# Splitting the mixed attention values a unit later, from tiles loaded a unit ahead, and one decay row loaded later

## The chip, the cores and the metric

One NeuronCore of a Trainium2 chip runs the whole program. The metric is the device time of one execution in microseconds; the kernel before takes 1137.94 us (median of three runs, 1137.45 to 1139.55).

## The reference, cut to what matters

One decoder layer on 1024 tokens of width 1024. Eight heads of kind A attend in a sliding window, eight heads of kind B attend causally with a decay bias; both read one input projection, and both results go through one output projection. A squared-ReLU MLP follows.

```python
xn = rmsnorm(x, attn_norm_g)
proj = einsum('bsd,de->bse', xn, w_in)            # q, k, v of both kinds, forget logits
out_a = swa_sinks_attention(qa, ka, va, sinks)     # 8 heads, window 128
c = cumsum(log_sigmoid(f_logit + b_forget))        # one decay row of 1024 values per B head
p = softmax(causal(qb @ kb.T * scale + c[q] - c[k]))
out_b = p @ vb                                     # 8 heads
x = x + concat([out_a, out_b]) @ w_out
x = x + square(relu(rmsnorm(x) @ w_up)) @ w_down
```

## The kernel before

**Arithmetic.** Every matmul operand is split in two parts, high and low, and three products (high-high, high-low, low-high) stand for one. `split` (line 73) makes the parts: ACT casts the high part, POOL or DVE subtracts it.

**Stages.** (1) The projection of the first columns; (2) attention: eight A heads in 16 units of work, then the B heads in pairs p = 0 to 3, eight units each (u = 0 to 3 the first head of the pair, 4 to 7 the second); (3) the output projection; (4) the up products and the down products of the MLP. This change lies in stage 2 from the B heads on and in the first products of stage 3.

**A unit.** `scores_b` (line 604) makes the score products (`spb`) on PE, adds the decay row (`cb`) on DVE (line 626) and takes the exponential on ACT. `mix_b` (line 650) comes two units later (`DEPTH` = 2): PE transposes the probabilities (`tpb`), ACT and DVE evict them as `pth` (line 359) and `ptl` (line 360), PE multiplies them by the values (`pvb`), and DVE adds the two halves of the sum into `mtb` (line 679). For p < 3 the sum is not yet divided by its softmax denominator and goes to DRAM (`mix_d`). For p = 3 it is divided before and split directly into `mix7`.

**Mixed values.** `split_mix(e)` (line 556) finishes one pair e of the concatenated heads: for each half c of 512 tokens SP loads the sum (`mixr`) and the inverse denominators (`mixn`), DVE multiplies them (line 565), ACT and POOL split the product (`mixs`), and SP writes the parts to `mixs_d`. `SPLITS` (line 49) says behind which unit (p, u) each of the seven pairs e = 0 to 6 is started. `load_mix(e)` (line 777) reads a finished pair back as `mix0` to `mix6` for the output projection. Each of `mixr`, `mixn` and `mixs` has one buffer.

**Fillers.** The projections of later pairs (`ps` products) and the first halves of the output projection (`out_first`, `po` products of `mix0` to `mix3`) are laid between the units by `PACE`. After the last unit the program loads pair 6, multiplies pairs 4, 5 and 6 (lines 831 to 835), finishes the last two units (`drain(0)`) and multiplies pair 7. `out_finish` then adds the first halves and makes the operands of the MLP.

**Order.** The kernel is built with a scheduler that orders each engine's instructions by dependencies and priorities; each engine then runs its list in order, SP's list of transfers too. Inside `with tc.issue_after(i)` an instruction is placed behind i on its engine. `prep` gives a high priority.

**Decay rows.** `prep_k(p, h)` (line 594) makes the keys of head h and loads its decay row `cb`; it is called for h = 1 at the last unit of the pair before. There are two buffers of `cb`.

Of the kernel before, what the change touches and what calls it, by code (L numbers as in the profile page):

```python
# [8 lines left out]
F32 = mybir.dt.float32  # L9
# [3 lines left out]
ALU = mybir.AluOpType  # L13
# [3 lines left out]
P = 128  # L17
D = 1024
S = 1024
KT = D // P  # L20
NT = S // P
HD = 64
# [31 lines left out]
def hybrid_layer(  # L54
# [501 lines left out]
    def split_mix(e):  # L556

        for c in range(2):
            cs = slice(c * 512, (c + 1) * 512)
            m, q = (ap2.tile([P, 512], F32, tag=n, name=n, bufs=1) for n in ("mixr", "mixn"))  # L560
            hl = ap2.tile([P, 2, 512], F32R, tag="mixs", name="mixs", bufs=1)
            nc.sync.dma_start(m, mix_d[e][:, cs])
            for h in range(2):
                nc.sync.dma_start(q[rows_of[h], :], rd_d[2 * e + h, cs].partition_broadcast(HD))
            nc.vector.tensor_tensor(out=m, in0=m, in1=q, op=ALU.mult)
            split(hl[:, 0], hl[:, 1], m, nc.scalar, nc.gpsimd)
            nc.sync.dma_start(
                mixs_d[e][:, :, cs].rearrange("c p s -> p c s"), hl.bitcast(F32)
            )

# [23 lines left out]
    def prep_k(p, h):  # L594
        heads[p, "k1", h] = make_k_b(qkb[p], P, p, h)
        cb = ap2.tile([P, S], F32, tag="bias", name=f"cb{p}{h}", bufs=2)
        nc.sync.dma_start(cb, c_d[2 * p + h].partition_broadcast(P))
        heads[p, "cb", h] = cb
# [51 lines left out]
    def mix_b(probs, p, qp, h):  # L650
# [28 lines left out]
        nc.vector.tensor_tensor(out=mt[r, :], in0=pv[:HD, :256], in1=tmp[:, :256], op=ALU.add)  # L679
# [53 lines left out]

    def heads_b(p):
        for u in range(8):
            qp, h = (ORDER_END if p == 3 and u > 3 else ORDER_B)[u % 4], u // 4
            unit(lambda: scores_b(p, qp, h), lambda got, qp=qp, h=h: mix_b(got, p, qp, h))
            if u == DEPTH:
                prep(prep_v, p, 1)
                if p:  # L740
                    prep(inverse_to, 6 + 2 * p, dn_b[(p - 1) % 2], 2)
                else:
                    prep(inverse_a)
            if (p, u) in SPLITS:
                split_mix(SPLITS.index((p, u)))
            ahead(p + 1, u)
            fill()
# [191 lines left out]
    def up(j):  # L939
# [3 lines left out]
        s = slot(("m5", "m4")[j % 2], "wus", [4, 4, P])  # L943
# [180 lines left out]
    def h_add(c, dt, cs):  # L1124

        nset[1] += 1
        h = slot(("m3", "m5")[nset[1] % 2], "hy", [4, 512])
# [117 lines left out]
```

## Time and profile before

| | us |
|---|---|
| runs of before | 1137.94 median (1137.45 to 1139.55) |
| the profiled execution | 1135.57 |
| its span | 1133.8 |
| PE busy | 1105.2 (97%) |
| DVE busy | 767.8 (68%) |
| ACT busy | 574.4 (51%) |
| POOL busy | 383.4 (34%) |

The profiled execution is 2.4 us under the median. A busy PE is not a PE at its rate: a matmul that starts alone shows its whole latency as busy, one in a stream overlaps with the next, so the number of PE instructions in equal stretches says more than the busy share. The stretch that matters here runs from 215 us, where the first inverse denominators are ready, to 465 us, where the output projection begins to run without waits.

### The profile page before, as it was taken

How to read it: one execution, taken by the hardware profiler on the slowest of the kernel's cores; microseconds unless marked ns; L12 is line 12 of the kernel's file. 1: busy time of each engine (PE TensorE's matmuls, PEld its weight loads, DVE VectorE, ACT ScalarE, POOL GpSimd, SP SyncE). 2: the span in 40 equal slices, each digit the busy share in tenths (PEclk: the TensorE clock that was granted, in tenths of full speed). 3: DMA queues.
4: the chain of work that ended last, by engine and by line, in shares of the span. 5: the costliest groups of instructions: out<-in, count | busy, mean ns of one | idle time of the engine just before them, and what ended most of it. 6: DMA issues, size and time to landing. Idle time of an engine off the chain costs nothing.

```text
span 1133.8 us, 15566 instructions
## 1 busy us (share of the span) xinstructions
PE 1105.2 (97%) x5551; PEld 937.0 (83%) x5551; DVE 767.8 (68%) x1307; ACT 574.4 (51%) x1013; POOL 383.4 (34%) x342
## 2 busy tenths in 40 slices
PE   9999999989999999999999999999999999999998
PEld 8999987888997887787888887888888888888876
DVE  7476665766558577798867677856575877674493
ACT  5567567666557666545454534344443433333330
POOL 5751513345324634133332322222222222231241
PEclk9999999999999999999999999999999999999999
DMA  9311301355307647363554544335699786665441
GB/s 314 117 43 29 94 20 54 94 170 167 105 27 294 196 166 258 124 231 130 186 195 168 194 149 154 141 119 200 227 391 347 265 303 233 230 232 183 167 149 38
DMA packets 95710, 195.68 MB, mean 173 GB/s; under 512 B 7136, under 2 KB 19088, under 8 KB 95632
## 3 DMA queue, kind: packets, MB, share of 16 engines
q1 hardware_dynamic: 95488, 194.66, 49.0%
q8 instruction: 44, 0.72, 0.3%
q14 instruction: 34, 0.28, 0.1%
q10 hardware_dynamic: 144, 0.02, 0.0%
HBM read 141.61 MB, written 53.04 MB: 172 GB/s over the span
## 4 chain that ended last, share of the span: by engine, by line
PE 75%; DVE 9%; DMA 6%; issue 5%; POOL 3%; ACT 2%; SPq 0%; DVEq 0%; POOLq 0%; ACTq 0%
PE pd L71 27%; PE pu L71 26%; PE ps L71 6%; PE po L71 5%; PE qps L71 3%; DMA mixr<-mix_d 2%; PE pvb L71 2%; PE spb L71 2%; DVE ptl L360 1%; DMA h_d<-h 1%; PE sp L71 1%; PE tpb L662 1%; DVE sb L626 1%; POOL qkb L267 1%; DVE ss L241 1%
## 5 line engine op out<-in xcount | busy, mean ns | idle before, releaser
L71 PE MATMUL pd<-hx,wx 128*128 128x512 f32 x1344 | 306.8, 391 | 2.4 <-POOL wx L78 2.4
L71 PEld LDWEIGHTS pd<-hx,wx 128*128 128x128 f32 x1344 | 253.4, 189 | 55.7 <-POOL wx L78 2.8
L71 PE MATMUL pu<-bh,wu 128*128 128x512 f32 x896 | 281.9, 395 | 0.8 <-ACT bh L858 0.8
L71 PEld LDWEIGHTS pu<-bh,wu 128*128 128x128 f32 x896 | 168.3, 188 | 41.9 <-ACT bh L858 1.3
L71 PE MATMUL pu<-bl,wu 128*128 128x512 f32 x448 | 176.8, 395 | 0.1
L78 POOL TENSOR_TENSOR wx<-wda,wx 128x1024 fp32r<-128x1024 f32 x28 | 85.0, 3038 | 221.5 <-ACT wx L75 193.9
L75 ACT CAST hx<-hr 128x1024 fp32r<-128x1024 f32 x56 | 59.0, 1054 | 181.0 <-PE pd L71 175.8
L78 DVE TENSOR_TENSOR hx<-hr,hx 128x1024 fp32r<-128x1024 f32 x56 | 76.0, 1364 | 81.4 <-ACT hx L75 81.2
L71 PE MATMUL ps<-wh,xh 128*128 128x384 f32 (+1 forms) x320 | 110.3, 345 | 0.3 <-ACT qkb L582 0.3
L71 PE MATMUL ps<-wh,xl 128*128 128x384 f32 (+1 forms) x320 | 109.1, 342 | 0.0
L71 PE MATMUL ps<-wl,xh 128*128 128x384 f32 (+1 forms) x320 | 109.0, 341 | 0.0
L71 PEld LDWEIGHTS pu<-bl,wu 128*128 128x128 f32 x448 | 84.2, 188 | 21.0 <-DVE bl L78 0.8
L71 PE MATMUL po<-mix,wos 128*128 128x512 f32 x384 | 96.6, 398 | 2.3 <-ACT mix L75 0.8
L78 POOL TENSOR_TENSOR wu<-wus,wu 128x512 fp32r<-128x512 f32 x32 | 46.6, 1458 | 134.3 <-ACT wu L75 128.5
L71 PEld LDWEIGHTS po<-mix,wos 128*128 128x128 f32 x384 | 70.0, 188 | 17.6 <-ACT mix L75 1.5
L75 ACT CAST wu<-wus 128x512 fp32r<-128x512 f32 x64 | 39.0, 618 | 83.9 <-PE pu L71 75.7
L78 POOL TENSOR_TENSOR wu<-wur,wu 128x512 fp32r<-128x512 f32 x32 | 45.9, 1436 | 88.4 <-ACT wu L75 88.4
L926 DVE TENSOR_TENSOR ht<-hb 128x512 f32<-128x512 f32 x32 | 21.8, 722 | 67.0 <-ACT hb L981 67.0
L78 POOL TENSOR_TENSOR wl<-wr,wh 128x384 fp32r<-128x384 f32 (+1 forms) x47 | 50.0, 1075 | 50.0 <-ACT wh L75 38.6
L360 DVE TENSOR_TENSOR ptl<-tpb,pth 128x512 fp32r<-128x512 f32 (+1 forms) x80 | 50.2, 632 | 19.6 <-ACT pth L359 18.5
L75 ACT CAST wx<-wda 128x1024 fp32r<-128x1024 f32 x56 | 58.3, 1044 | 6.9 <-DMA wda<-in_w_d_dram 6.6
L71 PEld LDWEIGHTS ps<-wh,xh 128*128 128x128 f32 x320 | 60.4, 189 | 1.4 <-ACT qkb L582 0.6
(213 smaller groups left out, 2056.3 us busy)
## 6 DMA issues: line engine op xcount, KB each, us to landing
wda<-in_w_d_dram SPq DMA_DIRECT2D x34, 1024.0 KB, 8.5
hr<-hid_d SPq DMA_DIRECT2D x56, 512.0 KB, 5.8
wur<-in_w_u_dram SPq DMA_DIRECT2D x32, 512.0 KB, 4.4
hid_d<-ht SPq DMA_DIRECT2D x16, 1024.0 KB, 4.3
hid_d<-hb SPq DMA_DIRECT2D x16, 768.0 KB, 3.6
mixs_d<-mixs SPq DMA_DIRECT2D x14, 512.0 KB, 3.5
mix<-mixs_d SPq DMA_DIRECT2D x7, 1024.0 KB, 8.2
wr<-in_w_b_dram SPq DMA_DIRECT2D x32, 192.0 KB, 2.6
```

Of the source, the lines that this page charges most:

```text
L71: return nc.tensor.matmul(out, lhsT, rhs, start=start, stop=stop)
L75: hi_eng.copy(hi, src)
L78: lo_eng.tensor_tensor(out=lo, in0=src, in1=hi.bitcast(F32), op=ALU.subtract)
L241: nc.vector.tensor_reduce(out=ss, in_=sq[:, : n * w].rearrange("p (g d) -> p g d", d=HD), axis=AX.X, op=ALU.add,)
L267: nc.gpsimd.tensor_tensor(out=xt, in0=xt, in1=rv[:, t].unsqueeze(2).to_broadcast([P, na, HD]), op=ALU.mult)
L360: nc.vector.tensor_tensor(out=lo[:, cols], in0=pt[:, cols], in1=hi[:, cols].bitcast(F32), op=ALU.subtract)
L626: nc.vector.tensor_tensor_reduce(out=pr[:, c * 512 : c * 512 + n], in0=sp[:, :n], in1=cb[:, c * 512 : c * 512 + n], scale=1.0, scalar=3e38 ...
L662: nc.tensor.transpose(tp[:, c0 : c0 + P], probs[qi][:, kb * P : (kb + 1) * P], ident)
L926: eng.tensor_tensor(out=out, in0=a, in1=b, op=ALU.subtract)
```

## The change

`split_mix(e)` now returns three steps. `load` runs behind the unit of `SPLITS` and loads both halves, each into tiles of its own (two buffers of `mixr` and of `mixn`). `make(0)` runs behind the next unit and `make(1)` behind the one after; each multiplies, splits and writes one half, and the multiply is placed behind the sum `mtb` that was programmed last (`mixed[-1]`). `load_c(p, 1)`, the decay row of a pair's second head, moves from the last unit of the pair before to unit 1 of its own pair. Two later scratch tiles (`wus` of even j, one of the two `hy`) move to the pool `zr`, which opens after attention.

```diff
--- before.py
+++ after.py
@@ -555,18 +555,36 @@
 
     def split_mix(e):
 
-        for c in range(2):
-            cs = slice(c * 512, (c + 1) * 512)
-            m, q = (ap2.tile([P, 512], F32, tag=n, name=n, bufs=1) for n in ("mixr", "mixn"))
+
+        got = {}
+
+        def load():
+            for c in range(2):
+                cs = slice(c * 512, (c + 1) * 512)
+                m, q = got[c] = [
+                    ap2.tile([P, 512], F32, tag=n, name=n, bufs=2) for n in ("mixr", "mixn")
+                ]
+                nc.sync.dma_start(m, mix_d[e][:, cs])
+                for h in range(2):
+                    nc.sync.dma_start(
+                        q[rows_of[h], :], rd_d[2 * e + h, cs].partition_broadcast(HD)
+                    )
+
+        def make(c):
+            m, q = got[c]
             hl = ap2.tile([P, 2, 512], F32R, tag="mixs", name="mixs", bufs=1)
-            nc.sync.dma_start(m, mix_d[e][:, cs])
-            for h in range(2):
-                nc.sync.dma_start(q[rows_of[h], :], rd_d[2 * e + h, cs].partition_broadcast(HD))
-            nc.vector.tensor_tensor(out=m, in0=m, in1=q, op=ALU.mult)
+            with tc.issue_after(mixed[-1]):
+                nc.vector.tensor_tensor(out=m, in0=m, in1=q, op=ALU.mult)
             split(hl[:, 0], hl[:, 1], m, nc.scalar, nc.gpsimd)
             nc.sync.dma_start(
-                mixs_d[e][:, :, cs].rearrange("c p s -> p c s"), hl.bitcast(F32)
-            )
+                mixs_d[e][:, :, c * 512 : (c + 1) * 512].rearrange("c p s -> p c s"),
+                hl.bitcast(F32),
+            )
+
+        return [load, lambda: make(0), lambda: make(1)]
+
+
+    mixed = []
 
     def project_b(p):
         got = {}
@@ -593,9 +611,12 @@
 
     def prep_k(p, h):
         heads[p, "k1", h] = make_k_b(qkb[p], P, p, h)
-        cb = ap2.tile([P, S], F32, tag="bias", name=f"cb{p}{h}", bufs=2)
+        if h == 0:
+            load_c(p, 0)
+
+    def load_c(p, h):
+        cb = heads[p, "cb", h] = ap2.tile([P, S], F32, tag="bias", name=f"cb{p}{h}", bufs=2)
         nc.sync.dma_start(cb, c_d[2 * p + h].partition_broadcast(P))
-        heads[p, "cb", h] = cb
 
     def prep_v(p, h):
         c0 = 256 + h * HD
@@ -676,7 +697,10 @@
         tmp = ap2.tile([HD, 512], F32, tag="cmb", name="tmpb", bufs=1)
         nc.scalar.copy(tmp[:, :256], pv[HD:, :256])
         mt = ap2.tile([P, 256], F32, tag="mt", name="mtb", bufs=2)
-        nc.vector.tensor_tensor(out=mt[r, :], in0=pv[:HD, :256], in1=tmp[:, :256], op=ALU.add)
+        add = nc.vector.tensor_tensor(
+            out=mt[r, :], in0=pv[:HD, :256], in1=tmp[:, :256], op=ALU.add
+        )
+        mixed.append(add.ins)
         ms = slice(qp * 256, (qp + 1) * 256)
         if p < 3:
             nc.sync.dma_start(mix_d[4 + p, r, ms], mt[r, :])
@@ -731,18 +755,25 @@
                     prep(make_q_a, 1, g, j)
             fill()
 
+    splitting = []
+
     def heads_b(p):
         for u in range(8):
             qp, h = (ORDER_END if p == 3 and u > 3 else ORDER_B)[u % 4], u // 4
             unit(lambda: scores_b(p, qp, h), lambda got, qp=qp, h=h: mix_b(got, p, qp, h))
+            if u == 1:
+                load_c(p, 1)
             if u == DEPTH:
                 prep(prep_v, p, 1)
                 if p:
                     prep(inverse_to, 6 + 2 * p, dn_b[(p - 1) % 2], 2)
                 else:
                     prep(inverse_a)
+            for step in [st.pop(0) for st in splitting if st]:
+                step()
             if (p, u) in SPLITS:
-                split_mix(SPLITS.index((p, u)))
+                splitting.append(split_mix(SPLITS.index((p, u))))
+                splitting[-1].pop(0)()
             ahead(p + 1, u)
             fill()
 
@@ -940,7 +971,7 @@
         if 0 < j < NJ - 1:
             up_load(j + 1)
         raw = raws.pop(j)
-        s = slot(("m5", "m4")[j % 2], "wus", [4, 4, P])
+        s = slot(*(("m4", "wus", [4, 4, P]), ("m5", "wus", [4, 4, P], F32, "zr"))[j % 2 == 0])
         a11, a12, a21, a22 = raw[:, 0, :4], raw[:, 0, 4:], raw[:, 1, :4], raw[:, 1, 4:]
         plus(s[:, 0], a21, a22)
         minus(s[:, 1], s[:, 0], a11)
@@ -1124,7 +1155,7 @@
     def h_add(c, dt, cs):
 
         nset[1] += 1
-        h = slot(("m3", "m5")[nset[1] % 2], "hy", [4, 512])
+        h = slot(*(("m3", "hy", [4, 512]), ("m5", "hy", [4, 512], F32, "zr"))[nset[1] % 2])
         nc.sync.dma_start(h, h_d[dt : dt + 4, :, cs].rearrange("t p s -> p t s"))
         r = rr[:, cs].unsqueeze(1).to_broadcast([P, 2, 512])
         for d in (slice(0, 2), slice(2, 4)):
```

From `h<-po0` (line 868, now 899) on, all engines have their instructions in the same order as before; DVE, ACT and PE differ only between the first `mixr` and that place.

**DVE, units 6 and 7 of pair 0.** The rows from the first square sums (`ss`) of the next pair's normalisation on; `rqk` is the last of its chain, line 626 is now 647. Before:

```order
L241 TENSOR_REDUCE ss<-sq 128x16
L360 TENSOR_TENSOR ptl<-tpb,pth 128x512
L565 TENSOR_TENSOR mixr<-mixr,mixn 128x512
L246 SCALAR_TENSOR_TENSOR ss<-ss,ep_77 128x16
L626 ISA sb,nmb<-spb,cb_2295 128x512
L626 ISA nmb 128x1
L360 TENSOR_TENSOR ptl<-tpb,pth 128x512
L253 TENSOR_TENSOR su<-sr_2942 128x16
L626 ISA sb,nmb<-spb,cb_2295,nmb 128x384
L626 ISA nmb 128x1
L360 TENSOR_TENSOR ptl<-tpb,pth 128x384
```

Now:

```order
L241 TENSOR_REDUCE ss<-sq 128x16
L360 TENSOR_TENSOR ptl<-tpb,pth 128x512
L246 SCALAR_TENSOR_TENSOR ss<-ss,ep_77 128x16
L253 TENSOR_TENSOR su<-sr_2937 128x16
L254 TENSOR_TENSOR su<-su,ss 128x16
L261 SCALAR_TENSOR_TENSOR rqk<-su,sr_2937 128x4x4
L647 ISA sb,nmb<-spb,cb_2467 128x512
L647 ISA nmb 128x1
L360 TENSOR_TENSOR ptl<-tpb,pth 128x512
L360 TENSOR_TENSOR ptl<-tpb,pth 128x384
L647 ISA sb,nmb<-spb,cb_2467,nmb 128x384
```

No multiply stands inside the chain any more: the nearest one, of pair 0, follows the next sum `mtb`, twenty rows below the square sums. The four rows of the chain now follow each other.

**DVE and PE, the end of attention.** `mtb_5627` (before `mtb_5632`) is the sum of the third unit from the end, `mixr_5432` the second half of pair 6, `mix7` the split of the last pair. DVE before:

```order
L360 TENSOR_TENSOR ptl_5621<-tpb_5616,pth_5620 128x384
L360 TENSOR_TENSOR ptl_5669<-tpb_5664,pth_5668 128x384
L360 TENSOR_TENSOR ptl_5691<-tpb_5685,pth_5690 128x512
L679 TENSOR_TENSOR mtb_5632<-pvb_5576,tmpb_5630 64x256
L360 TENSOR_TENSOR ptl_5704<-tpb_5698,pth_5703 128x512
L679 TENSOR_TENSOR mtb_5680<-pvb_5663,tmpb_5678 64x256
L78 TENSOR_TENSOR mix7_4282<-mtb_5632,mix7_4282 64x256
L360 TENSOR_TENSOR ptl_5716<-tpb_5711,pth_5715 128x384
L78 TENSOR_TENSOR mix7_4282<-mtb_5680,mix7_4282 64x256
L679 TENSOR_TENSOR mtb_5727<-pvb_5684,tmpb_5725 64x256
```

DVE now:

```order
L360 TENSOR_TENSOR ptl_5616<-tpb_5611,pth_5615 128x384
L360 TENSOR_TENSOR ptl_5669<-tpb_5664,pth_5668 128x384
L360 TENSOR_TENSOR ptl_5691<-tpb_5685,pth_5690 128x512
L700 TENSOR_TENSOR mtb_5627<-pvb_5571,tmpb_5625 64x256
L577 TENSOR_TENSOR mixr_5432<-mixr_5432,mixn_5433 128x512
L360 TENSOR_TENSOR ptl_5704<-tpb_5698,pth_5703 128x512
L700 TENSOR_TENSOR mtb_5680<-pvb_5663,tmpb_5678 64x256
L78 TENSOR_TENSOR mix7_4282<-mtb_5627,mix7_4282 64x256
L360 TENSOR_TENSOR ptl_5716<-tpb_5711,pth_5715 128x384
L78 TENSOR_TENSOR mix7_4282<-mtb_5680,mix7_4282 64x256
L700 TENSOR_TENSOR mtb_5727<-pvb_5684,tmpb_5725 64x256
L78 TENSOR_TENSOR mix7_4282<-mtb_5727,mix7_4282 64x256
```

The second multiply of pair 6 now follows the sum of unit (3, 5); before it stood 46 rows ahead of that sum, and the first one 60 rows ahead.

PE before, where the products of pair 6 stand:

```order
L71 MATMUL pvb_5512<-pth_5518,vb31_5118 128x256
L71 MATMUL pvb_5512<-ptl_5519,vb31_5118 128x256
L71 MATMUL pvb_5512<-pth_5530,vb31_5118 128x256
L71 MATMUL po0_5643<-mix6_5636,wos_5640 128x512 x2
L71 MATMUL po1_5644<-mix6_5636,wos_5640 128x512 x2
L71 MATMUL po0_5643<-mix6_5636,wos_5640 128x512
L71 MATMUL po1_5644<-mix6_5636,wos_5640 128x512
L662 MATMUL tpb_5590<-ident_58,sb_5337 128x128 x2
L662 MATMUL tpb_5590<-ident_58,sb_5352 128x128 x2
L71 MATMUL pvb_5512<-ptl_5531,vb31_5118 128x256
```

PE now:

```order
L71 MATMUL pvb_5684<-pth_5715,vb31_5118 128x256
L71 MATMUL pvb_5684<-ptl_5716,vb31_5118 128x256
L71 MATMUL pvb_5684<-pth_5715,vb31_5118 128x256
L71 MATMUL pvb_5684<-ptl_5716,vb31_5118 128x256
L71 MATMUL po0_5643<-mix6_5636,wos_5640 128x512 x2
L71 MATMUL po1_5644<-mix6_5636,wos_5640 128x512 x2
L71 MATMUL po0_5643<-mix6_5636,wos_5640 128x512
L71 MATMUL po1_5644<-mix6_5636,wos_5640 128x512
L71 MATMUL po0_5643<-mix7_4282,wos_5640 128x512 x2
L71 MATMUL po1_5644<-mix7_4282,wos_5640 128x512 x2
L71 MATMUL po0_5643<-mix7_4282,wos_5640 128x512
L71 MATMUL po1_5644<-mix7_4282,wos_5640 128x512
```

The six products of pair 6 stood among the last units' transposes; now they stand behind the last `pvb` product, straight ahead of those of pair 7.

**SP, the same place.** `mixs_d` receives the split halves, `mix6` reads both back. Before:

```order
L779 DMA mix4_5486<-mixs_d_82 128x2x1024
L567 DMA mixs_d_82<-mixs_5439 128x2x512
L866 DMA h_5757<-part_d_83 128x1024
L779 DMA mix5_5488<-mixs_d_82 128x2x1024
L779 DMA mix6_5636<-mixs_d_82 128x2x1024
L818 DMA part_d_83<-xt_5447 128x1024
L786 DMA wor_5866<-in_w_o_dram 128x512
L866 DMA h_5804<-part_d_83 128x1024
```

Now:

```order
L810 DMA mix4_5476<-mixs_d_82 128x2x1024
L810 DMA mix5_5478<-mixs_d_82 128x2x1024
L849 DMA part_d_83<-xt_5437 128x1024
L817 DMA wor_5866<-in_w_o_dram 128x512
L897 DMA h_5804<-part_d_83 128x1024
L579 DMA mixs_d_82<-mixs_5536 128x2x512
L579 DMA mixs_d_82<-mixs_5631 128x2x512
L810 DMA mix6_5636<-mixs_d_82 128x2x1024
L900 DMA h_d_84<-h_5757 128x1024
```

Both writes of pair 6 moved behind the load of `h_5804`, directly ahead of the load of `mix6`.

## Rows read from the trace of the kernel before

**Rows 1.** Busy time of the engines in stretches (start:end in us, length, then busy us and instructions of PE, PEld, DVE, ACT, POOL, the granted clock, the DMA share, GB/s).

```profile
460.00:518.00 58.00, 55.63 (x236) 43.49 (x235) 51.36 (x71) 30.21 (x51) 19.84 (x11) 1.00 0.55 185
518.00:820.00 302.00, 301.94 (x1292) 242.72 (x1292) 209.33 (x301) 138.14 (x170) 87.24 (x61) 1.00 0.47 170
```

**Rows 2.** Waits between 195 and 465 us (engine line <- releaser: us in total, times, longest).

```profile
DVE mixr L565 <- DMA mixr<-mix_d: 17.2, 8, 4.3
...
DVE mixr L565 <- issue: 3.5, 3, 1.5
DVE ss L241 <- POOL sq L236: 3.0, 2, 1.5
DVE mixr L565 <- DMA mixn<-rd_d: 2.2, 2, 1.8
```

**Rows 3.** PE alone in stretches of 10 us (busy us and PE instructions, granted clock, DMA share, GB/s).

```profile
225.00:235.00 10.00, 10.00 (x69) 1.00 0.55 183
235.00:245.00 10.00, 9.04 (x60) 1.00 0.46 148
245.00:255.00 10.00, 7.99 (x54) 1.00 0.52 172
255.00:265.00 10.00, 9.43 (x63) 1.00 0.45 136
...
275.00:285.00 10.00, 8.37 (x52) 1.00 0.59 181
```

**Rows 4.** PE in order of time (start us, us, what, xcount, idle before and its releaser), the rows with idle time between 240 and 310 us.

```profile
244.28 0.38 PE L71 MATMUL pvb<-ptl,vb 128*128 128x256 f32 x1 [0.96 <-DVE ptl L360]
247.25 0.39 PE L71 MATMUL pvb<-pth,vb 128*128 128x256 f32 x1 [2.01 <-ACT pth L359]
264.15 0.52 PE L288 MATMUL ptk<-ident,qkb 128*64 128x128 f32 x3 [0.34 <-DVE ptl L360]
278.90 0.38 PE L71 MATMUL pvb<-ptl,vb 128*128 128x256 f32 x1 [0.19 <-DVE ptl L360]
280.78 0.39 PE L71 MATMUL pvb<-pth,vb 128*128 128x256 f32 x1 [0.29 <-ACT pth L359]
282.18 0.38 PE L71 MATMUL pvb<-ptl,vb 128*128 128x256 f32 x1 [1.01 <-DVE ptl L360]
304.05 0.44 PE L71 MATMUL spb<-k1b,q1b 128*128 128x384 f32 x1 [0.28 <-DVE nmb L626]
```

**Rows 5.** DVE in order of time, the multiplies next to those gaps.

```profile
245.22 0.69 DVE L565 TENSOR_TENSOR mixr<-mixr,mixn 128x512 f32<-128x512 f32 x1 [0.99 <-DMA mixr<-mix_d]
...
261.03 0.69 DVE L565 TENSOR_TENSOR mixr<-mixr,mixn 128x512 f32<-128x512 f32 x1 [4.35 <-DMA mixr<-mix_d]
...
277.30 0.94 DVE L565 TENSOR_TENSOR mixr<-mixr,mixn 128x512 f32<-128x512 f32 x1 [1.51 <-DMA mixr<-mix_d]
...
302.69 0.69 DVE L565 TENSOR_TENSOR mixr<-mixr,mixn 128x512 f32<-128x512 f32 x1 [4.26 <-DMA mixr<-mix_d]
```

**Rows 6.** SP's queue, waits between 195 and 465 us, and where the loads of `mix0` to `mix3` start; ACT's first cast of output weights.

```profile
SPq L597 <- DVE nmb L626: 15.3, 4, 11.7
...
SPq L779 <- PE ps L71: 3.2, 1, 3.2
...
341.62 2.09 SPq L779 DMA_DIRECT2D mix<-mixs_d  x4
...
357.87 0.60 ACT L75 CAST wos<-wor 128x512 fp32r<-128x512 f32 x1
```

**Rows 7.** DVE and ACT at the end of attention, in order of time: the sum of unit (3, 5) and the last cast of transposed probabilities.

```profile
457.98 0.42 DVE L679 TENSOR_TENSOR mtb<-pvb,tmpb 64x256 f32<-64x256 f32 x1
...
459.25 0.48 ACT L359 CAST pth<-tpb 128x384 fp32r<-128x384 f32 x1
```

**Rows 8.** The split of a half on ACT and POOL (xcount: ns min/median/max, first and last start), and the landing of the writes of `mixs`, us min/median/max.

```profile
L75 ACT CAST mixs<-mixr x14: 617/620/625, 223.9 to 431.9; 128x512 fp32r<-128x512 f32 x14
L78 POOL TENSOR_TENSOR mixs<-mixr,mixs x14: 1278/1289/1411, 224.6 to 432.6; 128x512 fp32r<-128x512 f32 x14
...
DMA to landing us min/median/max: 2.9/3.5/7.5
```

**Rows 9.** Landing of the seven loads of `mix`, us min/median/max; and the DMA engines at the end of attention (stretch, length, granted clock, DMA share, GB/s).

```profile
DMA to landing us min/median/max: 5.1/8.2/11.3
...
455.00:460.00 5.00, 1.00 0.00 0
460.00:465.00 5.00, 1.00 0.00 0
```

**Rows 10.** PE at the end of attention, in order of time.

```profile
449.75 1.68 PE L71 MATMUL po<-mix,wos 128*128 128x512 f32 x6 [0.72 <-DMA mix<-mixs_d]
...
461.03 0.28 PE L71 MATMUL pvb<-ptl,vb 128*128 128x256 f32 x1
...
464.98 5.29 PE L71 MATMUL po<-mix,wos 128*128 128x512 f32 x22 [0.31 <-DVE h L868]
```

**Rows 11.** The one gap of the down products on PE, and the granted clock around it (stretch, length, busy us and PE instructions, clock, DMA share, GB/s).

```profile
1105.81 23.20 PE L71 MATMUL pd<-hx,wx 128*128 128x512 f32 x94 [2.42 <-POOL wx L78]
...
1104.00:1108.00 4.00, 2.19 (x5) 0.74 0.38 140
1108.00:1112.00 4.00, 4.00 (x16) 0.84 0.00 0
```

## The prediction

> **What bounds the kernel now.** I read the stretches first: from 518 us on PE is busy without a gap (301.94 of 302 us) [rows 1], the change leaves the order of that work alone, and what PE loses before it is lost for good. So the question is how much PE idle time goes or comes between 215 and 465 us. There the second view, the waits, shows what the change aims at: DVE, which runs its list in order, stands 17.2 us for the loads of `mixr`, 3.5 us for nothing visible and 2.2 us for `mixn`, 22.9 us in all [rows 2]. But PE is the engine that sets the end, so the third view counts its instructions: 69 in 10 us where it runs freely, 60, 54, 63 and 52 in the four stretches next to multiplies [rows 3]. Its idle rows there add up to 5.1 us (0.96, 2.01, 0.34, 0.19, 0.29, 1.01, 0.28) [rows 4]. The 23 us of DVE are thus worth 5 to 7 us of PE at most.
>
> **The change part by part: the middle.** Four gaps of PE follow a multiply that waited. At 245.22 DVE waited 0.99 us for a load, and the chain of the normalisation (`ss`, then ACT, then the cast that PE waits 2.01 us for) stands behind it [rows 4, 5], as the list of the section on the change shows: this gap goes, since the multiply is no longer in that chain. The multiplies at 261.03 and 302.69 had waited 4.35 and 4.26 us; behind them PE lost 0.34 and 0.28 us, which go too. The gap of 0.96 us has the reduction `ss` as its near cause, and of the 1.49 us around 280 the multiply at 277.30 (1.51 us of waiting) is one cause beside the next normalisation; I take half of each, 0.5 and 0.75 us. Together 3.9 us. Against it, DVE's list now has the four rows of the normalisation chain one behind the other, so DVE itself waits for ACT's logarithm and exponential with score rows queued behind it. No row of before shows that arrangement; bounded by nothing and by the 1.5 us that DVE waited at most for the step ahead of that chain [rows 2], I take 0.6 us. So the middle gives 3.3 us. Its bounds are 0 (each gap is taken over by the next wait) and 6.8 us: the missing instructions of the four slow stretches against 69 are 9 + 15 + 6 + 17 = 47 [rows 3], times 10 / 69 us.
>
> The multiply (0.69 us), cast and subtraction are the same fourteen as before, so they cost nothing new. The decay row of the second head is loaded later: SP stood 15.3 us, once 11.7, for its buffer [rows 6], with stores and `mixr` loads queued behind. Now the buffer is free when the load comes up, and the row is wanted three units later. No PE row waits for it, so I book nothing beyond the gaps above. The two scratch tiles in `zr` are first used after attention has ended: nothing.
>
> **The start of the output projection.** SP now writes the first half of pair 4 ahead of the loads of `mix0` to `mix3`. Before, these began at 341.62 after 3.2 us of waiting for PE [rows 6], so most of the new wait hides there; what sticks delays the output weights behind those 4 MB, whose first cast at 357.87 stands ahead of exponentials on ACT. Between 0 and 2 us; I take 0.5, near the hidden end.
>
> **The end of attention.** This is the large term. The last half of pair 6 is now multiplied directly behind the sum of unit (3, 5), the third sum from the end, and PE's products of pair 6 stand behind the last `pvb`. From the start of that sum, t = 457.98 us before [rows 7]:
>
> - sum 0.42, multiply 0.69 [rows 5, 7]: ready at t + 1.1;
> - the cast stands on ACT behind the last transposed cast, which ended at 459.73 (459.25 + 0.48), t + 1.75 [rows 7]; 0.62 more gives t + 2.4;
> - subtraction on POOL 1.29: t + 3.7 [rows 8];
> - write to DRAM, 3.5 in the median, 2.9 at least: t + 7.2 [rows 8];
> - load of both parts, 1 MB: 5.1, 8.2, 11.3 us (least, median, most) [rows 9]. Those loads shared the DMA engines; here nothing else runs (share 0.00 from 455 to 465) [rows 9], so I take the least, 5.1: t + 12.3;
> - six products of pair 6 and six of pair 7, at 5.29 / 22 = 0.24 us each [rows 10]: 2.9, and 0.3 for the bank that DVE empties: t + 15.5.
>
> Before, free running began at 464.98, t + 7.0. The difference is 8.5 us. The sum itself comes earlier: the 0.72 us that PE waited for `mix6` and its six products (1.4 us) no longer stand ahead of it [rows 10], but the first half's multiply and cast do (up to 1.3, I take 1.0). That is 1.2 us earlier: 7.3 us remain.
>
> During this PE has nothing: its last `pvb` was issued at 461.03 [rows 10], t + 3.05, and `mix6` lands at t + 12.3, a gap of 9 us. What a gap does to the clock the trace shows once: after 2.42 us without work at 1105.81 the granted clock was 0.74 and 0.84 in the next two stretches of 4 us [rows 11], that is, part of them at 1.2 instead of 2.4 GHz, 0.26 x 4 + 0.16 x 4 = 1.7 us lost. I add these 1.7 us (nothing to 1.7 as bounds). End of attention: 9.0 us lost; with a write of 2.9, the cast hidden and the clock kept 5.7, with a load of 8.2 us 12.1.
>
> The Trainium skill, page "DMA: Bandwidth & Descriptors", section "Anatomy of one DMA — SWDGE (gpsimd) path", fits a transfer as about 2.0 us plus its bytes at 436 GB/s. By that, as an estimate, write and load would take 3.2 and 4.4 us and the end would cost 1.0 us less than by the rows, whose medians of 3.5 and 8.2 us are both slower and which SP issued, another path.
>
> **The sum.** -3.3 + 0.5 + 9.0 = +6.2 us. On the profiled execution's 1135.57 that is 1141.8; on the median, which lies 2.4 us above it, 1144.1. I forecast **1144 us**, slower.
>
> **Rivals.**
>
> *Faster: the loads hidden pay more than the end costs.* The middle gives its whole 6.8 us, the end costs its least, 5.7, and the output projection behind it gives back the 2.4 us that PE is idle from 460 to 518 (58.00 less 55.63) [rows 1], because DVE and POOL have run ahead during the gap: 1137.94 - 3.5 = 1134.4 us. It decides from the point where the end costs less than the middle and the projection return together. For it speaks that DVE's waits are many; against it that write, load and subtraction can't overlap, since the load waits for both writes. Chance 0.06. The Trainium skill speaks for this side: its page "Trainium Kernel Development and Optimization", section "Best Practices", asks to double-buffer so that transfers overlap with compute; the rows on DVE's waits agree that they did not overlap, but the rule says nothing of the last item, behind which there is no later work.
>
> *No difference.* The middle gives 5 to 6 us and the end costs 6 to 7 (clock kept, write at 2.9): 1137.94 + 1 = about 1139 us. For it: the gaps of rows 4 all stand next to multiplies; against it: the normalisation chains have causes of their own. Chance 0.15.
>
> *Slower still.* The load takes its median 8.2 us, the middle gives nothing because each gap passes to the next wait (cast, transposes), the start of the output projection costs 1 to 2: 1137.94 + 12.1 = about 1150 us. For it: all seven loads of `mix` before took at least 5.1; against it the idle DMA engines. Chance 0.17.
>
> That the change does not do what it says is excluded by the lists: the multiplies do stand behind the sums.
>
> **How the numbers follow.** Forecast (1141 to 1147.5) 0.62, slower still 0.17, no difference 0.15, faster 0.06. A measurement of this kernel can tell about 0.2%, 2.3 us: faster is below 1135.7, slower above 1140.2. Slower is 0.62 + 0.17 = 0.79. The range from 1138.5 to 1149.5 takes in the forecast, most of both neighbours, and leaves out the faster case and the worst of the slower one.
>
> **What would show it.** Right: a single gap of PE of 7 to 11 us ahead of the first product of `mix6`, released by its load; the granted clock below 1 behind it; the waits of DVE for `mixr` gone, and the PE count from 235 to 285 us higher by some 20 instructions. Wrong: PE reaching `mix6` with no gap over 4 us would break the forecast's sign; a gap as forecast with a total below 1140 would mean that the middle was worth more than PE's idle rows showed; new waits of DVE in the normalisation of more than 1 us each would mean that it was worth nothing.

## The result and the profile after

The changed kernel takes **1140.15 us** (median of 19 runs, 1137.71 to 1144.60) against 1137.97 us (19 runs): a ratio of 1.0023, 95% interval 1.0012 to 1.0034, or 2.6 us more (1.4 to 3.9). Timed a second time (g2, below) the ratio is 1.0017 (1.0008 to 1.0027). Ratios are of fast runs alone: one run of before (1355.09 us) and, below, one of e2 (1363.94 us) were in the slow state and stay out of them. So the change makes the kernel slower, as forecast, but by 2 to 2.6 us and not by 6.2.

| | before | after |
|---|---|---|
| median, us | 1137.97 | 1140.15 |
| profiled execution, us (its span) | 1135.57 (1133.8) | 1141.35 (1139.6) |
| PE busy, us | 1105.2 | 1103.8 |
| PE busy from 460 to 518 us [rows 1] | 55.63 of 58.00 | 52.09 of 58.00 |

The two profiled executions must not be compared by their end alone. At a row of PE ahead of the change (the second group of `ptk` behind 195 us, at 200.51 before and 204.26 after; called the second `ptk` below) the second one is already 3.75 us late, with the same order of work on PE up to there; a second trace of the kernel before (g1) is 4.08 us late at the same place. Times of two traces are therefore compared below from that row on.

**The middle.** PE alone in stretches of 10 us, after; columns as in [rows 3], which shows five of the same six stretches before (the sixth, 265 to 275, had 67):

```profile
225.00:235.00 10.00, 10.00 (x71) 1.00 0.21 60
235.00:245.00 10.00, 10.00 (x63) 1.00 0.04 9
245.00:255.00 10.00, 9.80 (x66) 1.00 0.13 41
255.00:265.00 10.00, 10.00 (x71) 1.00 0.54 165
265.00:275.00 10.00, 10.00 (x65) 1.00 0.50 145
275.00:285.00 10.00, 9.34 (x67) 1.00 0.40 125
```

The six counts add up to 403, against 365 before (an instruction on an edge counts in both stretches). These windows are not shifted by the 3.75 us. The same work is compared exactly from the second `ptk` to the group of `ptk` at 317.73 before and 314.89 after: the same 706 PE instructions lie between them, partly in another order (stretch, length, PE busy us and instructions, clock, DMA share, GB/s; before, then after):

```profile
200.51:317.73 117.22, 110.99 (x707) 1.00 0.41 127
```

```profile
204.26:314.89 110.63, 109.20 (x706) 1.00 0.34 103
```

That is 6.6 us less: PE's idle time fell by 4.8 us (6.2 to 1.4), and its busy time for the same instructions by 1.8. PE's rows with idle time from 240 to 315 us, after:

```profile
248.27 0.50 PE L71 MATMUL spb<-k1b,q1b 128*128 128x512 f32 x1 [0.20 <-DVE nmb L647]
...
280.85 0.39 PE L71 MATMUL pvb<-ptl,vb 128*128 128x256 f32 x1 [0.66 <-DVE ptl L360]
...
314.89 0.63 PE L288 MATMUL ptk<-ident,qkb 128*64 128x128 f32 x4 [0.30 <-DVE ptl L360]
```

1.2 us, of which 0.9 fall in the stretch of [rows 4], where 5.1 stood. DVE's multiplies (the tile `mixr`: count, ns least/median/most, first and last start) no longer have an idle row of DVE ahead of them; before, they had 22.9 us of it [rows 2]:

```profile
L577 DVE TENSOR_TENSOR mixr<-mixr,mixn x14: 673/693/1385, 254.0 to 452.9; 128x512 f32<-128x512 f32 x14
its engine sat idle before it (us, times) until:
who waited for it (us, times):
  ACT mixs L75: 3.0, 5
```

**The end of attention.** The chain of work that ended last, after, from the sum of unit (3, 5) on (start us, us, what); it answers to [rows 7 to 10]:

```profile
452.46 0.42 DVE mtb L700
...
452.91 0.50 DVE mixr L577
...
453.52 0.69 DVE ptl L360
...
454.30 0.63 ACT mixs L75
...
455.05 1.28 POOL mixs L78
...
456.35 2.74 DMA mixs_d<-mixs
...
459.23 4.89 DMA mix<-mixs_d
...
464.17 5.08 PE po L71 x11
...
469.27 1.30 DVE h L899 x2
```

PE's rows there, and the granted clock in stretches of 4 us (length, PE busy us and instructions, clock, DMA share, GB/s):

```profile
464.17 6.19 PE L71 MATMUL po<-mix,wos 128*128 128x512 f32 x14 [7.79 <-DMA mix<-mixs_d]
470.61 37.96 PE L71 MATMUL po<-mix,wos 128*128 128x512 f32 x166 [0.25 <-DVE h L899]
```

```profile
460.00:464.00 4.00, 0.00 (x0) 0.50 0.75 262
464.00:468.00 4.00, 3.83 (x9) 0.50 0.00 0
468.00:472.00 4.00, 3.75 (x12) 0.74 0.15 62
472.00:476.00 4.00, 4.00 (x20) 1.00 0.81 260
```

The gap is there as forecast: 7.79 us, released by the load of `mix6`. A clock of 0.50 is 1.2 of 2.4 GHz; the 14 products behind the gap took 0.44 us each, against the 0.24 of [rows 10].

### The profile page after: what moved, and what is told of

Same layout as the page of the kernel before. It is cut to its first block, busy times and chain, and to the rows that moved or that the text cites. A ratio compares the mean times of both kernels' runs of the same rounds, so it can differ in the third digit from the quotient of the medians.

```text
span 1139.6 us, 15582 instructions
## 1 busy us (share of the span) xinstructions
PE 1103.8 (97%) x5551; PEld 941.4 (83%) x5551; DVE 767.7 (67%) x1307; ACT 572.5 (50%) x1013; POOL 389.4 (34%) x342
## 4 chain that ended last, share of the span: by engine, by line
PE 80%; DVE 7%; DMA 6%; issue 4%; POOL 2%; ACT 2%; SPq 0%; ACTq 0%; POOLq 0%; DVEq 0%
PE pu L71 27%; PE pd L71 26%; PE ps L71 11%; PE po L71 5%; PE spb L71 3%; PE pvb L71 2%; PE tpb L683 2%; PE sp L71 1%; DMA xq<-in_x_dram 1%; DVE ptl L360 1%; DMA xr<-in_xT_dram 1%; DMA h_d<-h 1%; DMA wr<-in_w_b_dram 1%; PE pv L71 1%; PE tpa L519 1%
## 5 line engine op out<-in xcount | busy, mean ns | idle before, releaser
L78 POOL TENSOR_TENSOR wx<-wda,wx 128x1024 fp32r<-128x1024 f32 x28 | 90.5, 3232 | 216.1 <-ACT wx L75 216.1
L78 DVE TENSOR_TENSOR hx<-hr,hx 128x1024 fp32r<-128x1024 f32 x56 | 72.8, 1304 | 85.5 <-ACT hx L75 85.5
L71 PE MATMUL ps<-wh,xh 128*128 128x384 f32 (+1 forms) x320 | 110.6, 346 | 1.4 <-DVE z L416 1.1
L71 PEld LDWEIGHTS po<-mix,wos 128*128 128x128 f32 x384 | 72.5, 194 | 23.3 <-DMA mix<-mixs_d 8.0
```

What stands on the lines that cost most here:

```text
L71: return nc.tensor.matmul(out, lhsT, rhs, start=start, stop=stop)
L78: lo_eng.tensor_tensor(out=lo, in0=src, in1=hi.bitcast(F32), op=ALU.subtract)
```

## The experiments

Theory A, formed on these two traces: the middle gained about 7 us, twice what was forecast, and the end costs 9 to 11. Theory B: the middle gained 3.3 as forecast, and the end costs only 5 to 6 in net, because the work behind it takes back the rest. Theory C gives part of the difference to the scratch tiles. Ratios are to the kernel before in the same session; microseconds are the ratio less 1, times 1137.97. Diffs are cut to the lines that matter (`...`).

| run | what | median | ratio (95%) | us |
|---|---|---|---|---|
| e1 | pair 6 loaded at (3,3) | 1132.03 | 0.9956 (0.9942 to 0.9970) | -5.0 |
| e2 | before, pair 6 alone late | 1145.23 | 1.0068 (1.0050 to 1.0086) | +7.7 |
| e3 | after, pair 6 as before | 1130.93 | 0.9946 (0.9927 to 0.9965) | -6.1 |
| e4 | before, scratch tiles moved | 1137.19 | 0.9996 (0.9983 to 1.0008) | -0.5 |
| f1 | e3 without the tie to the sums | 1144.71 | 1.0062 (1.0048 to 1.0077) | +7.1 |
| f2 | e3 with one buffer | 1135.93 | 0.9985 (0.9971 to 0.9999) | -1.7 |
| f4 | after, gap filled with products | 1136.83 | 0.9988 (0.9978 to 0.9997) | -1.4 |
| g1 | before again | 1137.99 | 1.0006 (0.9993 to 1.0018) | +0.7 |
| g2 | after again | 1139.58 | 1.0017 (1.0008 to 1.0027) | +1.9 |
| h1 | pair 6 loaded at (3,4) | 1134.51 | 0.9976 (0.9959 to 0.9992) | -2.7 |
| h2 | pair 6 split into `mix6` on chip | 1130.43 | 0.9939 (0.9927 to 0.9951) | -6.9 |

**e1_last_pair_earlier.**

```diff
-SPLITS = (..., (2, 5), (3, 5))
+SPLITS = (..., (2, 5), (3, 3))
```

> The changed kernel, with the last pair (pair 6) loaded at unit (3,3) instead of (3,5), so that its halves are multiplied behind the sums seen at (3,4) and (3,5) and are long written when PE has done its last pvb. Theory A (the middle gained about 7 us, twice what was forecast, and the end of attention costs 9 to 11 us as forecast, its clock loss of 3 us among it): the 7.8 us gap and the low clock go, the time falls 9 to 10 us below the changed kernel, to 1130 to 1132 us, 0.994 of the kernel before. Theory B (the middle gained 3.3 us as forecast, and the end costs only 5 to 6 us in net, because the work behind it takes back the rest): 1134 to 1135.5 us, 0.997.

Measured 5.0 us below the kernel before (3.4 to 6.6), at the edge of A's range and within reach of B's end: alone it doesn't decide. The gap is gone; PE waits 0.95 us for `mix6` at 452.07 and the clock is 1.00 to 500 us.

**e2_late_last_pair_alone.** In outline; `split_late` is the change's `split_mix` with the three steps.

```diff
+            if (p, u) == SPLITS[6]:
+                splitting.append(split_late(6))
+                splitting[-1].pop(0)()
-            if (p, u) in SPLITS:
+            elif (p, u) in SPLITS:
                 split_mix(SPLITS.index((p, u)))
```

> The kernel before with one part of the change: pair 6 alone is loaded ahead and multiplied a unit later behind the sums (with the scratch tiles in zr, which make room for its tiles); the other six pairs stay as they were. Theory A: the whole cost of the end and nothing of the gain, 9 to 10 us above the kernel before, 1147 to 1148 us, with a gap of PE of 7 to 9 us and a granted clock of about 0.5 behind it. Theory B: 5 to 6 us above it, 1143 to 1144 us.

7.7 us slower (5.7 to 9.8): between the two, with the gap that A named:

```profile
469.02 5.52 PE L71 MATMUL po<-mix,wos 128*128 128x512 f32 x14 [7.63 <-DMA mix<-mixs_d]
```

**e3_old_last_pair.** For pair 6 load, `make(0)` and `make(1)` run at once at (3, 5), and its multiplies are not tied to a sum.

```diff
-            with tc.issue_after(mixed[-1]):
+            with tc.issue_after(mixed[-1]) if e < 6 else ExitStack():
...
```

> The changed kernel with pair 6 alone as before: loaded and multiplied at once at unit (3,5), in no tie to a sum. Theory A: the gain of the middle without the cost of the end, 6 to 8 us below the kernel before, 1130 to 1132 us. Theory B: 3.3 us below it, 1134.5 us. With e2 it says whether the two parts add up to the whole change (+2.2 us).

6.1 us faster than before (4.0 to 8.3): B's 3.3 is excluded, A's 7 is not. With e2 the parts add up to +1.6, the whole measured +1.9 to +2.6. The end costs 7.7 us by e2 and 8.8 by the difference of the changed kernel and e3.

**e4_scratch_tiles_alone.**

```diff
-        s = slot(("m5", "m4")[j % 2], "wus", [4, 4, P])
+        s = slot(*(("m4", "wus", [4, 4, P]), ("m5", "wus", [4, 4, P], F32, "zr"))[j % 2 == 0])
...
```

> The kernel before with only the two scratch tiles (wus of even j, hy of odd sets) moved into the pool zr. The order of all engines stays as it was; only some waits at the start of the up products fall on other tiles. Theories A and B: nothing, within 0.5 us of the kernel before. Theory C (the move of the tiles causes the 3.2 us that PE waits at the start of the up products in the changed kernel, 0.8 us before): 2 to 2.5 us slower, with that wait in its profile.

No difference, so C falls, though PE's wait at the start of the up products is long in its trace. In g1, the kernel before once more, it is long too (first row e4, second g1; 0.83 us in the first trace of before, 3.23 in that of after):

```profile
515.40 2.16 PE L71 MATMUL pu<-bh,wu 128*128 128x512 f32 x5 [3.59 <-ACT bh L858]
```

```profile
518.29 1.42 PE L71 MATMUL pu<-bh,wu 128*128 128x512 f32 x5 [2.74 <-ACT bh L858]
```

That wait varies from one execution to the next with the same program (0.83 and 2.74 us in the kernel before), and in e3, which has the moved tiles, it is 1.02 us: a long one does not need the change.

**The decay row** was not run, because there is nothing to run: put alone into the kernel before, or taken out of e3, its move leaves the lists of all five engines with their waits as they were, the load of `cb` on SP included. It can have no part in the time.

**f1_no_gate.**

```diff
-            with tc.issue_after(mixed[-1]) if e < 6 else ExitStack():
+            with ExitStack():
```

> The e3 kernel (the change with pair 6 as before) without the tie of the multiplies to a sum: the halves keep their own tiles and are loaded ahead, but DVE meets a multiply where the scheduler thinks that its loads have landed. Theory A1 (the gain of the middle, 6 us in e3, comes from where the multiplies stand in DVE's list): most of the gain is lost, 1135 to 1138 us, with waits of DVE for mixr or mixn of some 10 us in all. Theory A2 (it comes from the second buffer, which lets both halves load ahead): the gain is kept, 1130 to 1132 us.

13 us above e3, worse than A1 said. DVE meets the first eight multiplies, of four pairs, between 224 and 266 us, early again (in e3 between 251 and 326), and waits 18.1 us ahead of its fourteen multiplies in all, with scores and a normalisation queued behind. Up to the next `ptk` (the table at the end of this section) PE has already lost 10.5 us against e3. DVE, then PE (idle ahead of each in brackets):

```profile
234.00 0.69 DVE L577 TENSOR_TENSOR mixr<-mixr,mixn 128x512 f32<-128x512 f32 x1 [3.83 <-DMA mixr<-mix_d]
...
248.42 1.43 DVE L577 TENSOR_TENSOR mixr<-mixr,mixn 128x512 f32<-128x512 f32 x1 [3.05 <-DMA mixr<-mix_d]
```

```profile
235.15 0.50 PE L71 MATMUL spb<-k1b,q1b 128*128 128x512 f32 x1 [2.31 <-DVE nmb L647]
...
248.49 0.39 PE L71 MATMUL pvb<-pth,vb 128*128 128x256 f32 x1 [1.85 <-ACT pth L359]
250.62 0.39 PE L71 MATMUL pvb<-ptl,vb 128*128 128x256 f32 x1 [1.74 <-DVE ptl L360]
```

**f2_one_buffer.** One buffer for each of the two tiles, and each half loaded in its own `make`.

```diff
-                ap2.tile([P, 512], F32, tag=n, name=n, bufs=2) for n in ("mixr", "mixn")
+                ap2.tile([P, 512], F32, tag=n, name=n, bufs=1) for n in ("mixr", "mixn")
...
```

> The e3 kernel with one buffer again for mixr and mixn, so that the second half is loaded only when the first is multiplied; the multiplies keep their tie to the sums of two units. Theory A1: the second half has a unit's time to land, so the gain is kept, 1130 to 1132 us, and DVE waits for mixr 3 us or less. Theory A2: the gain is lost, 1135 to 1138 us.

1.7 us below the kernel before: 4.4 of e3's 6.1 are lost, as A2 said, while f1 went as A1 said. Neither alone holds: the whole gain needs both, the place behind the sum and loads that start early enough for it (f2 changes the buffer and starts the loads a unit later; which of the two costs the 4.4 us is not shown). The trace says where each counts. Up to the `ptk` at 313.61 f2 still has most of the gain (112.0 us where e3 took 110.7 and before 117.2), so there the place alone does nearly all of it. It loses 4.2 us more behind that row, half of it around 342 to 355 us, where PE waits 2.32 us and the granted clock falls (0.50 from 345 to 350 us, 0.77 in e3). Waits of DVE for the loads of `mixr`, in e3 none, are back in f2, with 2.7 us for `mixn` beside them:

```profile
DVE mixr L580 <- DMA mixr<-mix_d: 7.1, 5, 3.5
```

**f4_filled_gap.** 30 products that nobody reads are added, behind the last `pvb`.

```diff
...
+    idle = pa.tile([P, 512], F32, tag="sc", name="spb", bufs=2)
+    with tc.issue_after(lastpv[0].ins):
+        for _ in range(30):
+            mm(idle, w[0][:, 0, :], mh[5][:, :512], True, True)
+        out_products(po_first, w, [6, 7])
```

> The changed kernel with 30 products of 128x512 that nobody reads on PE in the gap at the end of attention (7.1 us at 0.236 us each), so that PE is never idle there. Theory A (about 3 us of the end are the clock: 14 products took 6.19 us behind the gap instead of 3.3): the granted clock stays at 1.00 and the time falls by 2.5 to 3 us below the changed kernel, to 1137 to 1138 us. Theory B (the low clock costs nothing in the end, since what stands behind it waits for other work anyway): 1140 us, as the changed kernel.

As A said, a little more: 4.0 us below the changed kernel (3.3 below g2; both were timed in other sessions, and by the intervals either could be 1.7 less or more). The 14 products take 3.49 us, and the clock stays at 1.00 (second fence, columns as above):

```profile
454.05 6.97 PE L71 MATMUL spb<-mix,wos 128*128 128x512 f32 x30
461.81 3.49 PE L71 MATMUL po<-mix,wos 128*128 128x512 f32 x14 [0.80 <-DMA mix<-mixs_d]
```

```profile
456.00:460.00 4.00, 4.00 (x20) 1.00 0.53 177
460.00:464.00 4.00, 3.20 (x14) 1.00 0.31 127
```

Its trace shows less. From the `pvb` at 352.52 free running begins 113.5 us on, against 116.0 in the changed kernel (`pvb` at 354.63) and 115.2 in g2 (351.13): 1.7 to 2.5 us, what the 14 products gain. Ahead of that row f4 had lost 1.2 us to a fall of the clock (0.83 from 340 to 350 us) that the two traces of the changed kernel do not have.

**g1_before_again.** No edit.

> The kernel before, unchanged, timed as one of the experiments: what two measurements of one program differ by, and a second trace of it. All theories: 1.000 within 0.15%. For the 0.8 us that PE waits at the start of the up products in its first trace (3.2 in the changed kernel's, 4.1 in e4's, whose order is that of the kernel before): if that wait is a matter of how the phases of DVE and POOL fall and not of the change, it comes out differently in this trace, anything from 1 to 4 us.

1.0006 (0.9993 to 1.0018). Its trace shows what the first one of this program didn't: behind two gaps of the middle the granted clock fell (PE's gaps, then stretches of 10 us, of g1):

```profile
248.42 0.38 PE L71 MATMUL pvb<-ptl,vb 128*128 128x256 f32 x1 [0.98 <-DVE ptl L360]
251.03 0.48 PE L71 MATMUL pvb<-pth,vb 128*128 128x256 f32 x1 [1.66 <-ACT pth L359]
...
308.60 0.44 PE L71 MATMUL spb<-k1b,q1b 128*128 128x384 f32 x1 [1.72 <-DVE nmb L626]
```

```profile
245.00:255.00 10.00, 7.36 (x40) 0.83 0.56 190
...
305.00:315.00 10.00, 8.28 (x43) 0.83 0.18 63
```

**g2_after_again.** No edit.

> The changed kernel, unchanged, once more: a second interval, and a second trace to set beside the first, whose start of attention came 3.7 us late for reasons ahead of the change. All theories: 1.002 +- 0.0015 of the kernel before. Theory A: the gap at the end of attention again 7 to 8.5 us, the granted clock 0.50 in it, and free running 18 us from the start of the sum of unit (3,5).

As expected: gap 7.70 us, and free running 17.3 us from the start of the sum (449.00 to 466.29), here with 5.00 us for the 14 products.

**h1_one_unit_earlier.**

```diff
-SPLITS = (..., (2, 5), (3, 5))
+SPLITS = (..., (2, 5), (3, 4))
```

> The changed kernel with pair 6 loaded at unit (3,4), between the changed kernel's (3,5) and e1's (3,3). The sums of (3,4) and (3,5) lie 5.1 us apart in the changed kernel's trace (447.35 and 452.46), so mix6 lands 5.1 us earlier, about 3 us after the last pvb instead of 7.8. Theory A (what the end costs is the chain of write and load after the last half, minus the work left on PE, plus the clock): 5 to 6.5 us below the changed kernel, 1133.5 to 1135.5 us. Theory B (any gap there costs the same, because the low clock is what hurts): 1138 to 1140 us.

1134.51 us, in A's range (4.6 to 5.3 below the changed kernel by the ratios); B (any gap costs the same) falls. 3.09 us of gap are left:

```profile
455.98 5.07 PE L71 MATMUL po<-mix,wos 128*128 128x512 f32 x14 [3.09 <-DMA mix<-mixs_d]
```

**h2_kept_on_chip.**

```diff
+            if e == 6:
+                cs = slice(c * 512, (c + 1) * 512)
+                split(mh[6][:, cs], ml[6][:, cs], m, nc.scalar, nc.gpsimd)
+                return
             split(hl[:, 0], hl[:, 1], m, nc.scalar, nc.gpsimd)
...
-    load_mix(6)
```

> The changed kernel with pair 6 at (3,5) as it is, but its split halves are written directly into mix6 on chip, without the write to DRAM (2.7 us in the trace) and the load back (4.9 us). Theory A (the round trip is the cost of the end): the second half is ready 3.9 us after the start of the sum, about when the last pvb ends; no gap over 1 us, the clock at 1.00, and the time is e1's and e3's or a little less, 1129 to 1132 us. Theory B (the late multiply itself, its cast and its subtraction are the cost): 1136 us or more.

As A said, and the lowest median of all, though not clear of e3: 6.9 us below the kernel before (5.6 to 8.3), 9.5 below the changed kernel (8.9 below g2, of the same session). The late multiply itself costs nothing that shows; the round trip through DRAM behind it does. From 449 us on PE's waits are under 0.5 us each, three of five for splits of `mix` tiles:

```profile
454.12 1.53 PE L71 MATMUL po<-mix,wos 128*128 128x512 f32 x5 [0.36 <-DVE mix L78]
456.09 1.20 PE L71 MATMUL po<-mix,wos 128*128 128x512 f32 x4 [0.43 <-DVE mix L78]
457.60 24.59 PE L71 MATMUL po<-mix,wos 128*128 128x512 f32 x107 [0.32 <-DVE h L905]
```

Measured inside the traces from the second `ptk`: to the `ptk` behind the middle (317.73 in the first trace of before), and to the row at which PE's output products run freely (us). In f1 and f2 two score products more stand ahead of the `ptk` behind the middle.

```
              ptk     next ptk   free     ptk to free   against before (264.47)
before      200.51    117.2     464.98    264.47
before, g1  204.59    118.6     469.68    265.09    +0.6
e4          201.50    116.7     464.35    262.85    -1.6
after       204.26    110.6     470.61    266.35    +1.9
after, g2   200.75    110.7     466.29    265.54    +1.1
e3          201.71    110.7     460.32    258.61    -5.9
e1          200.00    110.8     458.44    258.44    -6.0
h1          200.76    110.7     461.73    260.97    -3.5
h2          200.52    110.6     457.60    257.08    -7.4
e2          201.40    119.4     475.22    273.82    +9.4
f1          201.11    121.2     469.57    268.46    +4.0
f2          201.65    112.0     465.79    264.14    -0.3
f4          200.93    110.7     466.01    265.07    +0.6
```

The picture is that of the times, with a scatter: before, g1 and e4 have one order of work and differ by 2.2 us, so a difference of two single traces of that size shows nothing.

## Why the prediction was right in sign and wrong in size

**The middle: the step that failed.** "So the middle gives 3.3 us" was the mis-sized term of the sum. e3, the change without its late end, gives 6.1 us (4.0 to 8.3) by the timed runs and 5.9 in its trace, the start of the output projection included; ahead of that start the traces show 6.6. With 6.1 in place of the 3.3 and the 0.5 the forecast's sum is -6.1 + 9.0 = +2.9 us, inside the measured 1.4 to 3.9 (0.9 to 3.1 in g2). Two things made the term small.

First, the measure. I summed PE's idle rows, closed 3.9 us of them, and kept the count of missing instructions as a far bound. On the same 706 instructions PE's idle time fell by 4.8 us, though not gap by gap: those of 0.96 and around 280 us closed further than the halves that I gave them, and a small new one came. But 1.8 us more lay in rows that count as busy (110.99 us against 109.20). A part of it is what a restart costs: in f4's trace the `pvb` behind a wait starts at 452.10 and the next at 452.32 and 452.44, so the first takes 0.22 us where 0.12 is the pace. The bound of 6.8 us, from [rows 3], was the better estimate. The text had named a sign of this, a gap as forecast with a total below 1140; the two timings, 1140.15 and 1139.58, stand at its edge. From 235 to 285 us the count rose by 36, not by some 20.

Second, the 0.6 us that I took off for the normalisation chain, its four rows now back to back. After, DVE waits 1.2 us in two rows for ACT's step of that chain, and a score row stands behind the longer wait, as I feared; but PE's wait for that score, at 248.27, is only 0.20 us:

```profile
246.89 0.18 DVE L253 TENSOR_TENSOR su<-sr 128x16 f32<-128x16 f32 x1 [1.01 <-ACT sr L252]
...
247.52 0.69 DVE L647 CUSTOM_DVE_ANT_0 sb<-spb,cb 128x512 f32<-128x512 f32 x1
```

The clock is not needed for the gain: it stayed at 1.00 over these rows in the first trace of before and in that of after, and 6.6 us lie between them. It can add to it, which the forecast had no term for. In the three other traces with before's order in this stretch it fell: g1 and e2 have 0.97 over it, e4 0.99. In none of the seven with the changed order did it fall there (110.6 to 110.8 us each), though in e3 and f4 it did behind PE's wait of 1.72 us for `pvb` at 342 us (0.83 from 340 to 350). Over the timed runs the mean granted clock is much the same, 0.9957 (23 runs of before) and 0.9960 (6 of e3), so most of the 6.1 us is not the clock.

**The start of the output projection** was booked at 0.5 us and not tested alone. In the traces the gain, counted from the second `ptk`, is 6.6 us at the `ptk` behind the middle (317.73 before, 314.89 after) and 5.9 at the score product behind the start of the projection (352.74 and 350.57): 0.7 us are lost between, most of it in one wait of `pvb`, 1.72 us against 1.12.

**The end: right in sum, not in each part.** Forecast 9.0 us lost; measured 7.7 (e2) and 8.8 (changed kernel against e3), 7.7 in those two traces. e2's trace is 9.4 us late, but 2.2 of that were lost by the `ptk` behind the middle, and 7.2 are the end's. The chain held almost to the step: multiply t + 0.5, cast t + 1.8, POOL t + 2.6, ready for the write at t + 3.9, load issued at t + 6.8, first product at t + 11.7 (forecast t + 12.3), free running at t + 18.15 where t + 17.2 was forecast with the clock. h2, which leaves out the write and the load, confirms that these two are the cost. Two parts erred against each other. The clock was booked at 1.7 us, with 1.7 as its upper bound, from a gap of 2.42 us [rows 11]; f4 makes it 3.3 to 4.0 by the times and 1.7 to 2.5 in the traces, with 1.5 to 2.7 on the 14 products, so 1.7 was at best just enough; by how much it was too low stays open. And the sum of unit (3, 5) came earlier than the 1.2 us I allowed: it stands 9.3 us earlier from `ptk`, 5.9 of that by the middle, so 3.4. I had charged the multiply and cast ahead of it with 1.0 us, which does not show; without that charge 2.1 would have been allowed, so 1.3 of the 3.4 I cannot place.

The Trainium skill, page "DMA: Bandwidth & Descriptors", section "Anatomy of one DMA — SWDGE (gpsimd) path", gave an estimate of 7.6 us for write and load; the trace has 2.74 + 4.89 = 7.63 us, with no other transfer from 455 to 465 us. The sum agrees, while each part differs by half a microsecond (3.2 and 4.4 by the page), and this path is SP's.

**The decay row** was booked at nothing, which holds, for a reason that I had wrong: I expected SP's 15.3 us of waiting [rows 6] to go. SP waits longer there, 30.9 us in all after, and the edit by itself changes no list. That longer wait costs PE nothing that shows: the middle gained all the same. **The scratch tiles** cost nothing, as booked (e4).

**The rivals.** "No difference" had the middle nearly right (5 to 6 us) and the end slightly low; the truth lies between it and the forecast. The measured 1140.15 us lies inside the stated range because that range took in this rival, not because the sum was right. The faster rival fell because its condition (end cheaper than the middle) is met only when pair 6's late chain is taken out or shortened: e1, e3 and h2 are that rival made real. Two sums of the prediction do not come out: the least of the end, 5.7, is 6.0 by its own parts (9.0 less 1.7 for the clock, 0.6 for the write and 0.7 for the cast), and "slower still" names 1 to 2 us for the output projection that its 12.1 leaves out. The forecast uses neither.

Not settled: whether f4 gains anything beyond the 14 products, where its times and its trace differ, and what makes up the 1.8 us of the middle beyond the idle time in detail.

## What to carry to other kernels

A wait ahead of the bounding engine was better priced here by how many of its instructions are missing from a stretch (bound 6.8 us, measured 6.6) than by its idle rows (5.1), which leave out what each restart costs; best is the time between two rows with the same instructions between them. Loading ahead and placing the consumer later belong together: the late place with loads that start late gave 1.7 us here, loads ahead without the late place lost 7, both gave 6. And a pipeline that delays every item by a unit must treat the last item apart, since behind it nothing covers the chain: against the change as it stands, two units earlier were worth 7 us, and no trip through DRAM 9.

## What the hardware showed unexpectedly

Of two executions of the same program one kept the granted clock at 1.00 behind gaps of 0.96 and 2.01 us close together, in the other it was 0.83 in the stretch of 10 us with 0.98 and 1.66 us at the same place. So one trace without a fall is no proof that gaps of this length are free. What it costs is not fixed either: e4, with one fall in that stretch, ran it in 116.7 us, the first trace of before, with none, in 117.2. The profiled executions of the kernel before lie 2.4 us under and 5.5 us over the medians of their runs. Behind the 7.8 us gap the clock was 0.50 until 468 us, 4 us after PE had work again, and 1.00 from 472; in g2 it was back at 1.00 from 464, 3.4 us after. Filling the gap with work for nothing made the kernel faster, by 3.3 to 4.0 us in the times and 1.7 to 2.5 in the traces.
